# A bank of its own for the gate and up chunks, the last columns in three tiles, and a longer range of shifted ring places

## The chip, the cores and the metric

The kernel runs on one core of a Trainium2 chip. Its time is the device time in microseconds, as the median of the runs. The profile shows one execution, engine by engine: TensorE (PE, its weight loads PEld), VectorE (DVE), ScalarE (ACT), GpSimd (POOL) and the queues that issue transfers (SP, POOL).

## The reference

Two layers work on x, 256 tokens by 1024 columns in float32. Each has a token mixer (a projection to stick-breaking attention, block attention and two gates, a projection of each branch, a merge and an output projection), a residual and a LayerNorm, and then SwiGLU, a residual and a LayerNorm:

```python
def swiglu(x, w_gate, w_up, w_down):
    return (jax.nn.silu(x @ w_gate) * (x @ w_up)) @ w_down

for l in range(DEPTH):
    mix = hybrid_mixer(x, w_in[l], w_branch_sb[l], w_branch_moba[l], w_out[l])
    x = layer_norm(DEEPNORM_ALPHA * x + mix, ln_mix_g[l], ln_mix_b[l])
    ffn = swiglu(x, w_ffn_gate[l], w_ffn_up[l], w_ffn_down[l])
    x = layer_norm(DEEPNORM_ALPHA * x + ffn, ln_ffn_g[l], ln_ffn_b[l])
```

The inner width of SwiGLU is 2816, 22 chunks of 128.

## The kernel before

**Numbers in two parts.** A float32 value is kept as a rounded part (hi) and the remainder (lo), and a product is three matmuls: hi by hi, hi by lo, lo by hi (`mm3`, L493). The weights come in granules of 128 by 1024. For each, a transfer brings it to a buffer called raw, ScalarE's cast writes hi into the ring `whi`, and VectorE's subtraction writes lo into the ring `wlo`. A few granules per layer are loaded into the rings by GpSimd's queue.

**The rings.** Each ring has ten places of 1024 columns (`NSPLIT`); granule g goes to place g mod 10. The table `STATIONARY` (L303) lists ranges of granules whose place begins 16 columns later in `whi` and 48 columns later in `wlo` (`ON`). A granule can only be written when the work that read the last one in its place is done. The granules of layer 1 start at 136: 180 to 183 are its second branch projection (tiles l1pb), where the weights are the stationary operand, and 184 to 191 its output projection (l1pw), where they are the moving one. In layer 0 the same weights are granules 44 to 47 and 48 to 55, and the range (24, 50) holds 44 to 49.

**PSUM.** Eight banks of 512 columns, in three pools with two places each: M and C with one bank a place, B with two. A tile takes a place from its pool once its former tile's readers are done. Waits are kept by tile: a matmul that writes a tile waits for those who read it earlier, in whichever of its halves.

**SwiGLU's main loop.** After eight chunks that are computed ahead, seven rounds follow in each layer. A round computes two more chunks of gate and up (`h_chunk`, 48 matmuls of 256 columns each), and seven products of a 128-by-512 block of the down projection. These are a scheme that replaces eight products by seven; their sums p1, p5, p6 and p7 are combined at the end (`combine_line`), the other three add into `acc[0]` and into the first half of `acc[1]`. The order on TensorE in a round: p1, `acc[0]` twice, the even chunk, p5, p7, `acc[1][:, 0]`, p6, the odd chunk. Both chunks are computed into the same bank, `single`, which is the second half of `acc[1]`. After each chunk ScalarE takes gate and up out of it into a tile called sf (two instructions, in `activated`), and VectorE multiplies them and forms the sums that the products need.

**After the loop** the last chunks of the down projection (eight granules, `TAIL`) are added for tokens 0 to 127 (t = 0) into `acc[0]`, then for t = 1 into `acc[1]`, and a LayerNorm follows for each (`norm_line`, in the last layer `last_norm`). In the last layer, t = 1 goes column piece by column piece: 512 columns in the first half of `acc[1]`, 256 in the second half, 256 in a tile of C. After each piece VectorE adds it to x.

**The order of the work.** A planner in the code (`Weave`) records the instructions of all engines in one run through the program; it sets the place of the side work (weight splits, evacuations) by estimated times. On the chip each engine takes its instructions in that order and waits on semaphores.

Of the kernel before, what the change touches and what calls it, by code (L numbers as in the profile page):

```python
# [14 lines left out]
P = 128  # L15
DEPTH = 2
D = 1024
S = 256
# [8 lines left out]
ALPHA = (2 * DEPTH) ** 0.25  # L27
# [12 lines left out]
class Weave:  # L40
# [12 lines left out]
    def act(self, e, n, f, *args, **kw):  # L53
        f(*args, **kw)  # L54
        self.act_t = max(self.act_t, e) + n / 1200.0 + ACT_FIXED
        return self.act_t + HOP

    def dve(self, e, n, f, *args, **kw):
        f(*args, **kw)  # L59
        self.dve_t = max(self.dve_t, e) + n / 960.0 + DVE_FIXED  # L60
        return self.dve_t + HOP

    def pool(self, e, f, *args, **kw):
        f(*args, **kw)
        self.pool_t = max(self.pool_t, e) + 0.55
        return self.pool_t + HOP
# [38 lines left out]
class WeightStream:  # L105
# [62 lines left out]
    def _place(self, g):  # L168
        if SLOTS[g][0] == B11:
            return "half"  # L170
        if SLOTS[g][0] == B2X:
            return "off"
        return "on" if any(a <= g < b for a, b in STATIONARY) else "off"

# [125 lines left out]
NSPLIT = 10  # L300
ON = (16, 48)
HALF_AT = 256
STATIONARY = ((8, 20), (24, 50), (64, 130), (144, 180), (200, 260))  # L303
TURNED = ("l0sb3", "l1sb3")
N_WARM = 7
LEAD = 4
# [16 lines left out]
def hybrid_trunk_kernel(ctx: ExitStack, tc: tile.TileContext, w, xT_in, x_in, ln_in,  # L323
# [27 lines left out]
    def bankM(name, shape):  # L351
        return psM.tile(shape, F32, tag="M", name=name)

    def bankC(name, shape):
        return psC.tile(shape, F32, tag="C", name=name)

    def bankB(name, shape):
        return psB.tile(shape, F32, tag="B", name=name)

    weave = Weave()  # L360
    taken, left = [0], {}

    def turn(e):

        was = None
        while True:
            k = taken[0] - 2
            if k >= 0 and k not in left:
                yield
            elif (e := max(e, left.get(k, 0.0))) == was:  # L370
                break
            else:
                was = e
                yield e + MARGIN
        taken[0] += 1
        return taken[0] - 1
# [26 lines left out]
    def split_line(hi, lo, src, n, e):  # L403
        e = act(e, n, nc.scalar.copy, hi, src)
        yield e
        return dve(e, n, nc.vector.tensor_sub, lo, src, hi.bitcast(F32))
# [52 lines left out]
    e = dve(3.6, 512, nc.vector.tensor_copy, hi, ws.raw[0][:, first[0]])  # L459
# [39 lines left out]
    def transpose(o, a):  # L499
        nc.tensor.transpose(o, a, ident)  # L500
        weave.t += 0.11

    def pe_after(e):
        weave.t = max(weave.t, e)

    def pe_done():
        return weave.t + HOP
# [53 lines left out]
    def token_out(o, g, t, s_hi, s_lo, first, last):  # L561

        hi, lo = ws.take(g)
        ts = slice(t * P, (t + 1) * P)
        for c0, ps in o:
            cs = slice(c0, c0 + ps.shape[-1])
            mm3(ps, s_hi[:, ts], s_lo[:, ts], hi[:, cs], lo[:, cs], first, last)
# [257 lines left out]
    halves = [slice(h * 512, (h + 1) * 512) for h in range(2)]  # L825

    def residual(e, x, cs, ps, sum_out=None, scale=ALPHA, op=OP.add):
        return dve(e, cs.stop - cs.start, nc.vector.scalar_tensor_tensor, x[:, cs], x[:, cs], scale, ps,
                   op0=OP.mult, op1=op, accum_out=sum_out)

    def scale_shift(e, x, cols, sub, op, scale, g, b, e_scale):

        for c in cols:
            dve(e, c.stop - c.start, nc.vector.scalar_tensor_tensor, x[:, c], x[:, c], sub, g[:, c],
                op0=op, op1=OP.mult)
        for c in cols:
            e = dve(e_scale, c.stop - c.start, nc.vector.scalar_tensor_tensor, x[:, c], x[:, c], scale,
                    b[:, c], op0=OP.mult, op1=OP.add)
            yield c, e

    def norm_line(name, t, junk, gb, scale=ALPHA):

        x = xs[t]
        st = small.tile([P, 2], F32, tag="st", name=f"{name}_st{t}")
        nmu = small.tile([P, 1], F32, tag="nmu", name=f"{name}_nmu{t}")
        ve = small.tile([P, 1], F32, tag="ve", name=f"{name}_ve{t}")
        e = pe_done()
        for h in range(2):
            e = residual(e, x, halves[h], junk[:, h, :], st[:, h:h + 1], scale)
        e = dve(e, 16, nc.vector.tensor_scalar, nmu, st[:, 0:1], st[:, 1:2], -1.0 / D, op0=OP.add, op1=OP.mult)  # L850
        e2 = act(e, D + 100, nc.scalar.activation, junk, x.rearrange("p (h c) -> p h c", h=2), AF.Square,
                 bias=nmu, accum_out=ve)
        e2 = pool(e2, nc.gpsimd.tensor_scalar, ve, ve, 1.0 / D, EPS, op0=OP.mult, op1=OP.add)
        e2 = pool(e2, nc.gpsimd.tensor_tensor, ve, ve, mhalf, op=OP.pow)
        ends = [e for _, e in scale_shift(e, x, halves, nmu, OP.add, ve, *gb, e2)]
        for h in range(2):
            i = yield from turn(ends[h])
            tp = bankC(f"{name}_tp{t}{h}", [P, 4, P])
            pe_after(ends[h])
            for j in range(4):  # L860
                transpose(tp[:, j, :], x[:, (4 * h + j) * P:(4 * h + j + 1) * P])
            ks = slice(h * 4, (h + 1) * 4)
            ts = slice(t * P, (t + 1) * P)
            e = pe_done()
            yield e
            left[i] = xT_ready[t] = yield from split_line(xT_hi[:, ks, ts], xT_lo[:, ks, ts], tp, 512, e)
# [23 lines left out]
    def load_gb(l, i):  # L890
        tiles = []
        for j in range(2):
            a = unit(f"ln{l}{i}{j}", [P, D])
            nc.sync.dma_start(a, ln_in[4 * l + 2 * i + j].partition_broadcast(P))
            tiles.append(a)
        return tiles


    norms = []
    for l in range(DEPTH):  # L900
        G = l * NS_LAYER
        L = f"l{l}"
# [18 lines left out]
        else:  # L921
            for t in range(2):
                weave.finish(norms[:t + 1])
                pe_after(xT_ready[t])
                for j, put in enumerate((put_v, put_q)):
                    ps = bankM(f"{L}pvq{j}{t}", [P, WIDTH])
# [98 lines left out]
        for i in range(4):  # L1025
            ps = bankM(f"{L}pa{i}", [P, 2, S])
# [14 lines left out]
        gb = load_gb(l, 0)  # L1041
# [28 lines left out]
        norms, acc = [], {}  # L1070
        for t, cs in ((0, range(KC)), (1, range(KC))):
            if t not in acc:
                acc[t] = bankB(f"{L}pw{t}", [P, 2, 512])
            for c in cs:
                if t == 0 and c == 4:
                    ws.reach(G + 54)
                    weave.finish(m_sides)
                weave.finish(m_sides[c:c + 1])
                token_out([(512 * h, acc[t][:, h, :]) for h in range(2)], G + 48 + c, t, *m_parts(c),
                          c == 0, c == KC - 1)  # L1080
                if t == 1:
                    ws.allow(G + 48 + NSPLIT + c)
            if c == KC - 1:
                norms.append(weave.start(norm_line(f"{L}a", t, acc[t], gb)))
# [55 lines left out]
        for t in range(2):  # L1140
            weave.finish(norms[:t + 1])
            pe_after(xT_ready[t])
            for j in range(2):
                ps = bankM(f"{L}pft{t}{j}", [P, 512])
# [25 lines left out]
        for c in range(NTOK_FC, LEAD_FC):  # L1170
            h_chunk(c, bankM(f"{L}pf{c}", [P, 2, S]), G + 56 + 2 * c)
        acc = [bankB(f"{L}pd{t}", [P, 2, 512]) for t in range(2)]
        single = acc[1][:, 1, :].rearrange("p (b c) -> p b c", b=2)
        turns = range(taken[0], taken[0] + 2)
        taken[0] += 2
        p1, p6 = (bankC(f"{L}pd{n}", [P, 512]) for n in ("one", "six"))
        p5, p7 = (bankM(f"{L}pd{n}", [P, 512]) for n in ("five", "seven"))

        def combine_line():

# [41 lines left out]


        gb = load_gb(l, 1)
        banks = [[(512 * h, a[:, h, :]) for h in range(2)] for a in acc]
        if l == DEPTH - 1:
            weave.finish(combined)
            banks[1][1:] = [(512, single[:, 0, :]), (768, bankC(f"{L}pe", [P, 512])[:, :256])]

        def h_parts(i):  # L1230
            return [h[:, i % 4, :] for h in (h_tok, h_rest)[i // 4]]

        norms = []
        for t in range(2):
            def down(part, t=t):
                for i in range(len(TAIL)):
                    if i == 6:
                        weave.finish(sides)
                    for c0, ps in part:
                        token_out([(c0, ps)], g + i, t, *h_parts(i), t == 1 and c0 >= 512 and i == 0,  # L1240
                                  i == len(TAIL) - 1)
                    if t == 1:
                        ws.allow(g + i + NSPLIT)
            if l < DEPTH - 1:
                down(banks[t])
                weave.finish(combined)
                norms.append(weave.start(norm_line(f"{L}b", t, acc[t], gb, 1.0)))
            else:
                last_norm(f"{L}b", t, banks[t], gb, down)
        weave.finish(norms[:1])  # L1250
# [85 lines left out]
```

## Time and profile before

| | |
|---|---|
| median of 3 runs | 719.88 us (719.54 to 720.37) |
| profiled execution, its own time | 719.56 us |
| its span | 717.8 us |
| granted TensorE clock, mean | 0.998 |
| busy: PE, PEld | 702.4 us (98%), 641.2 us (89%) |
| busy: DVE, ACT, POOL | 596.6, 424.8, 34.7 us |
| HBM read, written | 148.87 MB, 8.13 MB |

A row of the timeline is: start in us from the span's start, length in us, engine, source line, operation, tile written <- tiles read, shape, and in brackets the engine's idle time just before it with the engine and tile that ended it. Buffer numbers are left out in names, so l0pd is `acc[0]` or `acc[1]` of layer 0 and, in the profile before, also `single`. The tiles of p1, p5, p6 and p7 are l0pdone, l0pdfive, l0pdsix and l0pdseven. A row of the waits is: engine, tile and line that waited, for whom, us in total, times, longest. A row of the chain of waits is: start, length, engine, tile, line. Source line 487 is the helper for all matmuls, 54 and 59 those for ScalarE and VectorE. The length of a matmul includes the pipeline, so the distance between two starts tells TensorE's pace.

### The profile page before, as it was taken

The numbers are of one execution on the slowest core, as the hardware profiler recorded it, in microseconds if no ns is written. First come the engines' busy times: TensorE is split into PE (matmuls) and PEld (weight loads), VectorE is DVE, ScalarE is ACT, GpSimd is POOL, SyncE is SP. The second block draws the span as 40 slices with busy tenths as digits, with TensorE's granted clock in tenths as the row PEclk, the third lists the DMA queues.
The fourth block names the chain that finished last, engine by engine and source line by source line (L and its number), as shares of the span: only waits on it lengthen the run. The fifth ranks groups of instructions, "written<-read, shape, count | busy, mean of one in ns | idle before, by whom it ended". The sixth has DMA issues, their size and how long they took to land.

```text
span 717.8 us, 12728 instructions
## 1 busy us (share of the span) xinstructions
PE 702.4 (98%) x4897; PEld 641.2 (89%) x4897; DVE 596.6 (83%) x887; ACT 424.8 (59%) x651; POOL 34.7 (5%) x48
## 2 busy tenths in 40 slices
PE   9999999999999999999999999999999999999994
PEld 6889999998898888889889889999888999999984
DVE  5999887898888887888588987878879889999855
ACT  5766677755665555565356566677466556666710
POOL 0001110001000000000000111000010000000001
PEclk9999999999999999999999999999999999999999
DMA  8998899876675665657459597995758656656701
GB/s 291 345 332 243 238 243 254 278 275 227 201 244 171 188 199 192 198 194 252 146 177 350 173 255 220 244 277 178 251 196 257 213 168 210 210 176 205 256 9 59
DMA packets 63053, 157.83 MB, mean 220 GB/s; under 512 B 10896, under 2 KB 23184, under 8 KB 62992
## 3 DMA queue, kind: packets, MB, share of 16 engines
q1 hardware_dynamic: 58304, 142.07, 60.0%
q0 software_dynamic: 4544, 14.68, 9.1%
q8 instruction: 38, 0.62, 0.3%
q10 hardware_dynamic: 144, 0.26, 0.1%
q14 instruction: 23, 0.19, 0.1%
HBM read 148.87 MB, written 8.13 MB: 219 GB/s over the span
## 4 chain that ended last, share of the span: by engine, by line
PE 78%; issue 8%; DVE 7%; DMA 3%; ACT 2%; POOL 1%; SPq 1%; POOLq 0%; DVEq 0%; ACTq 0%
PE l1pd L487 15%; PE l0pd L487 10%; PE l1pg L487 6%; PE l0pg L487 6%; DVE wlo L59 3%; PE l0pqk L487 3%; PE l0pw L487 3%; PE l0pft L487 3%; PE l1pw L487 3%; PE l1pft L487 3%; PE l0pf L487 3%; PE l1pf L487 3%; DMA raw<-in_w_dram 3%; PE l1pb L487 2%; PE l0pk L487 2%
## 5 line engine op out<-in xcount | busy, mean ns | idle before, releaser
L59 DVE TENSOR_TENSOR wlo<-raw,whi 128x1024 fp32r<-128x1024 f32 (+1 forms) x262 | 299.0, 1174 | 23.4 <-ACT whi L54 22.3
L54 ACT CAST whi<-raw 128x1024 fp32r<-128x1024 f32 (+1 forms) x261 | 256.7, 1016 | 50.2 <-DVE raw L59 30.3
L487 PE MATMUL l1pd<-xT_hi,whi 128*128 128x256 f32 x224 | 62.1, 277 | 0.0
L487 PE MATMUL l1pd<-xT_hi,wlo 128*128 128x256 f32 x224 | 62.1, 277 | 0.0
L487 PE MATMUL l1pd<-xT_lo,whi 128*128 128x256 f32 x224 | 62.0, 277 | 0.0
L487 PE MATMUL l0pd<-xT_hi,whi 128*128 128x256 f32 x224 | 62.0, 277 | 0.0
L487 PE MATMUL l0pd<-xT_hi,wlo 128*128 128x256 f32 x224 | 62.0, 277 | 0.0
L487 PE MATMUL l0pd<-xT_lo,whi 128*128 128x256 f32 x224 | 62.0, 277 | 0.0
L487 PEld LDWEIGHTS l1pd<-xT_hi,whi 128*128 128x128 f32 x224 | 42.1, 188 | 0.6
L487 PEld LDWEIGHTS l1pd<-xT_lo,whi 128*128 128x128 f32 x224 | 42.1, 188 | 0.6
L487 PEld LDWEIGHTS l0pd<-xT_hi,whi 128*128 128x128 f32 x224 | 42.0, 188 | 0.6
L487 PEld LDWEIGHTS l0pd<-xT_lo,whi 128*128 128x128 f32 x224 | 42.1, 188 | 0.6
L487 PEld LDWEIGHTS l1pd<-xT_hi,wlo 128*128 128x128 f32 x224 | 42.1, 188 | 0.0
L487 PEld LDWEIGHTS l0pd<-xT_hi,wlo 128*128 128x128 f32 x224 | 42.1, 188 | 0.0
L487 PE MATMUL l1pg<-xT_hi,whi 128*128 128x256 f32 x128 | 35.8, 279 | 0.4 <-DVE l1vmb L59 0.4
L487 PE MATMUL l0pg<-xT_hi,whi 128*128 128x256 f32 x128 | 35.7, 279 | 0.0
L487 PE MATMUL l0pg<-xT_hi,wlo 128*128 128x256 f32 x128 | 35.4, 277 | 0.0
L487 PE MATMUL l1pg<-xT_hi,wlo 128*128 128x256 f32 x128 | 35.4, 277 | 0.0
L487 PE MATMUL l0pg<-xT_lo,whi 128*128 128x256 f32 x128 | 35.4, 277 | 0.0
L487 PE MATMUL l1pg<-xT_lo,whi 128*128 128x256 f32 x128 | 35.4, 276 | 0.0
L59 DVE TENSOR_TENSOR l0sf<-l0sf 128x256 f32<-128x256 f32 (+1 forms) x32 | 11.7, 364 | 17.1 <-ACT l0sf L54 16.6
L487 PEld LDWEIGHTS l1pg<-xT_hi,whi 128*128 128x128 f32 x128 | 24.0, 188 | 1.3 <-DVE l1vmb L59 0.9
(487 smaller groups left out, 2028.0 us busy)
## 6 DMA issues: line engine op xcount, KB each, us to landing
raw<-in_w_dram SPq DMA_DIRECT2D x226, 512.0 KB, 4.9
whi<-in_w_dram POOLq DMA_DIRECT2D x14, 512.0 KB, 6.1
wlo<-in_w_dram POOLq DMA_DIRECT2D x14, 512.0 KB, 8.1
ln<-in_ln_dram SPq DMA_DIRECT2D x8, 512.0 KB, 7.3
raw<-in_w_dram SPq DMA_DIRECT2D x7, 256.0 KB, 5.2
l0mb_scr<-l0mb_turn SPq DMA_DIRECT2D x4, 384.0 KB, 6.9
l0mb_turn<-l0mb_scr SPq DMA_DIRECT2D x16, 96.0 KB, 5.2
l1mb_scr<-l1mb_turn SPq DMA_DIRECT2D x4, 384.0 KB, 4.6
```

Of the source, the lines that this page charges most:

```text
L54: f(*args, **kw)
L59: f(*args, **kw)
L487: nc.tensor.matmul(o, a, b, start=start, stop=stop)
```

## The change

`single` becomes an M tile of its own (`bankM`, named pf). p7, which had an M place, goes to the second half of `acc[1]`; p5 stays in M. Before, t = 1 had its second 512 columns in `acc[1]`'s second half; now they are in `single`, in both layers. So `norm_line` is given the two tiles that it reads, and in the last layer the three pieces lie in three tiles. The range (144, 180) becomes (144, 190), so granules 180 to 189 are shifted too.

```diff
-STATIONARY = ((8, 20), (24, 50), (64, 130), (144, 180), (200, 260))
+STATIONARY = ((8, 20), (24, 50), (64, 130), (144, 190), (200, 260))
...
-    def norm_line(name, t, junk, gb, scale=ALPHA):
+    def norm_line(name, t, junk, gb, scale=ALPHA, sums=None):
...
         for h in range(2):
-            e = residual(e, x, halves[h], junk[:, h, :], st[:, h:h + 1], scale)
+            e = residual(e, x, halves[h], sums[h] if sums else junk[:, h, :], st[:, h:h + 1], scale)
...
         acc = [bankB(f"{L}pd{t}", [P, 2, 512]) for t in range(2)]
-        single = acc[1][:, 1, :].rearrange("p (b c) -> p b c", b=2)
+        single = bankM(f"{L}pf", [P, 2, S])
...
-        p5, p7 = (bankM(f"{L}pd{n}", [P, 512]) for n in ("five", "seven"))
+        p5, p7 = bankM(f"{L}pdfive", [P, 512]), acc[1][:, 1, :]
...
-        banks = [[(512 * h, a[:, h, :]) for h in range(2)] for a in acc]
+        flat = single.rearrange("p b c -> p (b c)")
+        banks = [[(0, a), (512, b)] for a, b in ((acc[0][:, 0, :], acc[0][:, 1, :]), (acc[1][:, 0, :], flat))]
         if l == DEPTH - 1:
             weave.finish(combined)
-            banks[1][1:] = [(512, single[:, 0, :]), (768, bankC(f"{L}pe", [P, 512])[:, :256])]
+            banks[1][1:] = [(512, flat[:, :256]), (768, bankC(f"{L}pe", [P, 512])[:, :256])]
...
-                norms.append(weave.start(norm_line(f"{L}b", t, acc[t], gb, 1.0)))
+                norms.append(weave.start(norm_line(f"{L}b", t, acc[t], gb, 1.0, [ps for _, ps in banks[t]])))
```

The order of instructions is the same on every engine. What differs is which tile they name, and which of them wait. Rows of the order name an instruction's line, operation, tile written <- tiles read and shape, and the semaphores of engines that it waits for.

TensorE in the first round of layer 0, from p5's last matmul to the odd chunk's first, before:

```order
L487 MATMUL l0pdfive<-whi,l0hp_lo 128x512
L487 MATMUL l0pdseven<-whi,l0hp_hi 128x512 [waits Activation_49]
L487 MATMUL l0pdseven<-wlo,l0hp_hi 128x512
L487 MATMUL l0pdseven<-whi,l0hp_lo 128x512
L487 MATMUL l0pd_2565<-whi,l0hp_hi 128x512 [waits Activation_49]
L487 MATMUL l0pd_2565<-wlo,l0hp_hi 128x512
L487 MATMUL l0pd_2565<-whi,l0hp_lo 128x512
L487 MATMUL l0pdsix<-whi,l0hp_hi 128x512
L487 MATMUL l0pdsix<-wlo,l0hp_hi 128x512
L487 MATMUL l0pdsix<-whi,l0hp_lo 128x512
L487 MATMUL l0pd_2565<-xT_hi,whi 128x256
```

and with the change:

```order
L487 MATMUL l0pdfive<-whi,l0hp_lo 128x512
L487 MATMUL l0pd_2565<-whi,l0hp_hi 128x512
L487 MATMUL l0pd_2565<-wlo,l0hp_hi 128x512
L487 MATMUL l0pd_2565<-whi,l0hp_lo 128x512
L487 MATMUL l0pd_2565<-whi,l0hp_hi 128x512
L487 MATMUL l0pd_2565<-wlo,l0hp_hi 128x512
L487 MATMUL l0pd_2565<-whi,l0hp_lo 128x512
L487 MATMUL l0pdsix<-whi,l0hp_hi 128x512
L487 MATMUL l0pdsix<-wlo,l0hp_hi 128x512
L487 MATMUL l0pdsix<-whi,l0hp_lo 128x512
L487 MATMUL l0pf<-xT_hi,whi 128x256 [waits Activation_49]
```

The wait on ScalarE has moved from `acc[1][:, 0]`'s product (the fifth row before) to the first matmul of the odd chunk (the last row), six matmuls later. p7 now writes `acc[1]` (2565) too.

TensorE at the boundary of the layers, where t = 1's last sums are followed by layer 1's first two tiles (l1pvq00 and l1pvq10), before:

```order
L487 MATMUL l0pd1_2565<-wlo_99,l0hr_hi_3467 128x512
L487 MATMUL l0pd1_2565<-whi_98,l0hr_lo_3468 128x512
L487 MATMUL l1pvq00_3899<-whi_98,xT_hi_108 128x512 [waits Activation_49]
...
L487 MATMUL l1pvq00_3899<-wlo_99,xT_hi_108 128x512
L487 MATMUL l1pvq00_3899<-whi_98,xT_lo_109 128x512
L487 MATMUL l1pvq10_3929<-whi_98,xT_hi_108 128x512
L487 MATMUL l1pvq10_3929<-wlo_99,xT_hi_108 128x512
```

and with the change (three of l1pvq00's 24 matmuls are shown, the first and the last two):

```order
L487 MATMUL l0pf_2566<-wlo_99,l0hr_hi_3467 128x512
L487 MATMUL l0pf_2566<-whi_98,l0hr_lo_3468 128x512
L487 MATMUL l1pvq00_3899<-whi_98,xT_hi_108 128x512 [waits Activation_49]
...
L487 MATMUL l1pvq00_3899<-wlo_99,xT_hi_108 128x512
L487 MATMUL l1pvq00_3899<-whi_98,xT_lo_109 128x512
L487 MATMUL l1pvq10_3929<-whi_98,xT_hi_108 128x512 [waits DVE_49]
L487 MATMUL l1pvq10_3929<-wlo_99,xT_hi_108 128x512
```

l1pvq00's wait is as before. l1pvq10 now waits for VectorE, whose last read of `single` (l0pf) frees the place in M.

TensorE at the end of layer 1, where the second column piece of t = 1 begins, before:

```order
L487 MATMUL l1pd1_6276<-whi_98,l1hr_hi_7173 128x512
L487 MATMUL l1pd1_6276<-wlo_99,l1hr_hi_7173 128x512
L487 MATMUL l1pd1_6276<-whi_98,l1hr_lo_7174 128x512
L487 MATMUL l1pd1_6276<-whi_98,l1h0_hi_5814 128x256 [waits DVE_49]
L487 MATMUL l1pd1_6276<-wlo_99,l1h0_hi_5814 128x256
L487 MATMUL l1pd1_6276<-whi_98,l1h0_lo_5815 128x256
```

and with the change:

```order
L487 MATMUL l1pd1_6276<-whi_98,l1hr_hi_7173 128x512
L487 MATMUL l1pd1_6276<-wlo_99,l1hr_hi_7173 128x512
L487 MATMUL l1pd1_6276<-whi_98,l1hr_lo_7174 128x512
L487 MATMUL l1pf_6277<-whi_98,l1h0_hi_5814 128x256
L487 MATMUL l1pf_6277<-wlo_99,l1h0_hi_5814 128x256
L487 MATMUL l1pf_6277<-whi_98,l1h0_lo_5815 128x256
```

The piece is written to `single` (l1pf), and the wait on VectorE is gone.

## The prediction

> **What bounds the kernel now.** I read the page's first part, then TensorE's waits, then the chain of waits, and last the timelines where TensorE stops.
>
> ```profile
> PE 702.4 (98%) x4897; PEld 641.2 (89%) x4897; DVE 596.6 (83%) x887; ACT 424.8 (59%) x651; POOL 34.7 (5%) x48
> ...
> PE l0pd L487 <- ACT l0sf L54: 4.8, 6, 1.0
> PE l1pd L487 <- DVE x L59: 1.5, 1, 1.5
> ...
> PE l1pg L487 <- DVE l1vmb L59: 0.4, 1, 0.4
> ```
>
> TensorE is the bound: it is busy for 98% of the span, and apart from the start only two waits are worth money. Six times in layer 0 it waits until ScalarE has evacuated a gate-and-up chunk into l0sf, and once at the very end until VectorE has updated x. Idle time counts from the modelled end of a pipelined matmul, so each wait costs more than that view says; start-to-start times tell the price. First, the layer-0 wait in rounds one and two:
>
> ```profile
> 228.27 0.40 PE L487 MATMUL l0pdseven<-whi,l0hp_lo 128*128 128x512 f32 x1
> 229.69 0.50 PE L487 MATMUL l0pd<-whi,l0hp_hi 128*128 128x512 f32 x1 [1.03 <-ACT l0sf L54]
> 230.03 0.40 PE L487 MATMUL l0pd<-wlo,l0hp_hi 128*128 128x512 f32 x1
> 230.26 0.39 PE L487 MATMUL l0pd<-whi,l0hp_lo 128*128 128x512 f32 x1
> ...
> 245.35 0.40 PE L487 MATMUL l0pdseven<-whi,l0hp_lo 128*128 128x512 f32 x1
> 246.49 0.50 PE L487 MATMUL l0pd<-whi,l0hp_hi 128*128 128x512 f32 x1 [0.75 <-ACT l0sf L54]
> 246.82 0.40 PE L487 MATMUL l0pd<-wlo,l0hp_hi 128*128 128x512 f32 x1
> ```
>
> A 512-column matmul follows the last after 0.23 us (230.03 to 230.26). The waiting one comes after 1.42 us and its successor after 0.34 us, so round one loses 1.76 - 0.46 = 1.30 us; round two loses 1.14 + 0.33 - 0.46 = 1.01 us. What TensorE waits for is seen in the chain of waits:
>
> ```profile
> 224.28 2.35 DVE wlo L59 x2
> 226.63 0.61 DVE raw L59
> 227.26 0.70 DVE raw L59
> ...
> 228.04 1.05 ACT whi L54
> 229.09 0.56 ACT l0sf L54 x2
> ...
> 229.69 0.96 PE l0pd L487 x3
> 230.65 0.69 PE l0pdsix L487 x3
> 231.34 5.51 PE l0pd L487 x48
> 236.88 0.04 issue
> 236.93 0.66 ACT l0sf L54 x2
> 237.61 0.44 DVE l0sf L59
> 238.07 0.43 DVE l0sf L59
> ```
>
> The even chunk's two evacuations stand in ScalarE's queue behind a cast that waits for VectorE's additions. The product acc[1][:, 0] (three matmuls) does not read what they write; it only writes the other half of the tile they read. It has to wait all the same, and p6 and the odd chunk (48 matmuls) stand behind it. Layer 1 does the same work without this wait:
>
> ```profile
> 238.50:322.50 84.00, 80.26 (x586) 74.11 (x585) 71.28 (x94) 49.36 (x73) 0.00 (x0) 1.00 0.58 188
> 591.40:670.40 79.00, 79.00 (x587) 74.55 (x586) 72.01 (x95) 49.38 (x71) 0.00 (x0) 1.00 0.60 200
> ```
>
> Columns: length, then busy time of TensorE, its weight loads, VectorE, ScalarE, GpSimd, granted clock, DMA share, GB/s. Five rounds take 84.0 us in layer 0 and 79.0 us in layer 1: 1.0 us each, as the start-to-start times said. TensorE runs at its full granted clock in both.
>
> **The change part by part.** *The chunk's own bank, in the loop.* The product acc[1][:, 0] loses its wait. The evacuation now holds up only the odd chunk, which really rewrites that bank; its first matmul stands six 512-column matmuls later (two products: 6 x 0.23 = 1.37 us). Is that enough cover? In round one TensorE reaches the odd chunk at 228.27 + 7 x 0.228 = 229.86, and the release that the chain shows is 229.69: 0.17 us to spare. In the others it reaches it at 245.35 + 1.59 = 246.94, against 246.49: 0.45 us. Does the release move when a round gets shorter? The chain runs from the odd chunk's evacuation (236.93) through VectorE's work on it, its splits and additions, and the cast, to the even evacuation, with no step of TensorE in between: from 236.88 to 246.49 it takes 9.6 us, and from there the odd chunk needs 236.88 - 231.18 = 5.7 us (its first matmul is below). A round by this chain is 15.3 us, under the 15.8 us that TensorE needs. So TensorE stays the bound, and the gain is 1.30 + 5 x 1.01 = 6.35 us, taken as 6.3. VectorE's work, 71.3 us in five rounds, fits 79.0 us, as layer 1 shows (72.0). Bounds: 6.4 if no remainder of the wait is left; 2.5 if one more cast of 1.05 us came ahead of each evacuation (0.88 us left in round one, 0.60 in each of the five others).
>
> ```profile
> 230.95 0.39 PE L487 MATMUL l0pdsix<-whi,l0hp_lo 128*128 128x512 f32 x1
> 231.18 0.28 PE L487 MATMUL l0pd<-xT_hi,whi 128*128 128x256 f32 x1
> ```
>
> That the other banks change (p7 into the freed half, p5 into the other M place) costs nothing: p7 is read by VectorE in the combination, and acc[1]'s next write comes after the whole t = 0 pass of 48 matmuls.
>
> *The end.* In the last layer the second third of x's last columns goes into that bank, and no longer waits for VectorE's read of the first:
>
> ```profile
> 702.35 0.39 PE L487 MATMUL l1pd<-whi,l1hr_lo 128*128 128x512 f32 x1
> 704.28 0.39 PE L487 MATMUL l1pd<-whi,l1h_hi 128*128 128x256 f32 x1 [1.55 <-DVE x L59]
> 704.51 0.28 PE L487 MATMUL l1pd<-wlo,l1h_hi 128*128 128x256 f32 x1
> ...
> 703.55 0.68 DVE L59 SCALAR_TENSOR_TENSOR x<-x,l1pd 128x512 f32<-128x512 f32 x1
> 704.26 0.69 DVE L59 BATCH_NORM_STATS2 l1b_bn<-x 128x6 f32<-128x512 f32 x1
> 707.45 0.42 DVE L59 SCALAR_TENSOR_TENSOR x<-x,l1pd 128x256 f32<-128x256 f32 x1 [2.49 <-PE l1pd L487]
> ```
>
> From 702.35 to the second 256-column matmul it takes 2.16 us; without the wait 0.23 + 0.12 = 0.35. VectorE does not take the gain away: it is done with the first piece at 704.95, and the second then comes at about 705.6 instead of 707.45. All that follows moves by 1.8 us.
>
> *The layer boundary.* x's second half of t = 1 is now read from the chunk's bank, an M place, and the next layer's first tiles are M tiles. The order shows that the added wait lies on l1pvq10, 24 matmuls into the layer, not on l1pvq00. VectorE's second read begins at 360.13 and takes 0.69 us; l1pvq10 starts at 364.75.
>
> ```profile
> 359.31 0.39 PE L487 MATMUL l1pvq<-whi,xT_hi 128*128 128x512 f32 x1
> 364.75 0.39 PE L487 MATMUL l1pvq<-whi,xT_hi 128*128 128x512 f32 x1
> ...
> 360.13 0.68 DVE L59 SCALAR_TENSOR_TENSOR x<-x,l0pd 128x512 f32<-128x512 f32 x1
> ```
>
> Cost nothing; the 24 matmuls hide it. Without them it would be 360.82 - 359.31 + 0.11 for the restart = 1.6 us.
>
> *The ring places.* Granules 180 to 189 move by 16 and 48 columns: 180 to 183 are layer 1's l1pb weights (stationary), 184 to 189 the first six of its w_out (moving). Layer 0's l0pb already sits in such places:
>
> ```profile
> 141.50 10.88 PE l0pb L487 x96
> 152.39 17.83 PE l0pw L487 x78
> ...
> 496.91 11.52 PE l1pb L487 x96
> 508.42 18.39 PE l1pw L487 x81
> ```
>
> The same 96 matmuls take 10.88 against 11.52 us: a gain of 0.64. The moving side pays a little. l0pw, with two of its eight granules shifted, runs at 17.83 / 78 = 0.2286 us, l1pw, with none, at 18.39 / 81 = 0.2270; 78 x 0.0016 = 0.12 us for two granules, so about 0.3 for six. Bounds: 0 to 0.4. Net 0.3 gained. The Trainium skill ("SBUF — State Buffer", Specifications) counts operands in lines of 16 bytes; shifts of 64 and 192 bytes keep every start's place in its line, so by that rule nothing moves here and the total is 0.3 us smaller. The rows of l0pb and l1pb differ, and I go by them.
>
> **The sum.** 6.3 + 1.8 + 0.3 = 8.4 us. The profiled execution took 719.56 us (span 717.8), which gives 711.2; the median of the runs is 0.3 above it. I predict 711.3 us.
>
> **The rivals.** *A, the wait only moves.* The chunks of a round still share one bank, so the odd chunk waits for the same evacuation, and only 0.17 to 0.45 us keep them apart. Should the evacuation come a cast later, the loop brings the lower bound of 2.5, the sum is 4.6 and the time 715.3. Against it: the chain of 15.3 us above. The Trainium skill ("Perfetto Trace Analysis", Matmuls) wants independent matmul groups to rotate through banks, so that an evacuation overlaps the next group; by it this rival is what to expect of one bank.
>
> *B, the gain is used up downstream.* TensorE arrives 6.3 us earlier at layer 1, where one wait (0.4 us, l1vmb) shows that VectorE is close behind. If weights bound that stretch, the loop's gain would be spent there and only 1.8 + 0.3 stay: 717.8. Against it: that is the only wait between the two loops, and loads and splits are released by TensorE's progress.
>
> *C, no change.* The waits are for data, not for the tile, and the layout alters nothing but the 0.3 of the ring: 719.6. Against it: the product reads l0hp and the ring, and layer 1, with the same reads, does not wait.
>
> *D, slower.* In layer 0's loop, VectorE and ScalarE become the bound: without TensorE's pause they meet casts that wait for ring places, ahead of the evacuation. The chain must grow from 15.3 us past 16.8 + 2.1 / 6 = 17.2 us before the 2.1 us from elsewhere are eaten; one further whi cast and wlo split in each (1.05 + 1.2 us) make 17.5, so 6 x 0.7 - 2.1 = 2.1 us slower, 722.0. Against it: VectorE is idle for 84.0 - 71.3 = 12.7 us of five rounds, and TensorE frees places earlier, not later.
>
> **How the numbers follow.** Forecast 0.80, A 0.11, B 0.03, C 0.03, D 0.03. The forecast's own range is 710.3 to 712.4 (ring and loop bounds, and 0.4 us between runs). To leave no more than 2 in 10 out I reach into A, as far as an evacuation three quarters of a cast late (0.6 + 5 x 0.34 = 2.3 us left, 713.6): 709.9 to 714.0. A measurement tells about 0.2% (1.4 us) from no change; forecast, A and B lie beyond it: faster 0.94, same 0.03, slower 0.03.
>
> **What would show it.** In the changed profile TensorE's waits hold no wait for l0sf before acc[1]'s product, five layer-0 rounds take 79 us, l1pf follows l1pd in the end without a gap, l1pb takes 10.9 us, and nothing stops before l1pvq. A wait of l0pf's odd chunk on l0sf would show A; a new wait for l1vmb or whi in layer 1, B; rounds over 16.8 us, D. The prediction is wrong if the evacuation falls behind the odd chunk's start.

## The result, and the profile after

The changed kernel takes 711.06 us (median of 4 runs, 710.88 to 711.3), the one before, on the same chip, 719.95 us (4 runs, 719.54 to 720.37). The ratio is 0.9877 with a 95% interval of 0.986 to 0.9894: 8.9 us faster. The prediction was 711.3 us. The profiled execution took 711.3 us, with a span of 709.5 us.

First the page's busy times after, and the first rows of TensorE's waits (engine, tile and line that waited, for whom, us in total, times, longest):

```profile
PE 700.5 (99%) x4897; PEld 642.3 (91%) x4897; DVE 595.9 (84%) x887; ACT 424.2 (60%) x651; POOL 34.7 (5%) x48
```

```profile
PE busy L441 <- DVE mhalf L436: 1.0, 1, 1.0
PE l1pg L487 <- DVE l1vmb L59: 0.3, 1, 0.3
```

Neither the six waits for l0sf nor the wait for x is there, and no row for l0pf or l1pvq has come in their place. What is left is a wait at the start (busy, before the first projection), one of 0.3 us in layer 1, which was 0.4 us before, and one of 0.2 us in the first projection (l0pv, for a cast).

Where did the time go? p1 is the first product of a round, so its first and last starts (two figures after the durations) bound six of the seven rounds. The rows are those of tiles l0pdone, l1pdone and l1pe, before and then after; l1pe is the last column piece.

```profile
L487 PE MATMUL l0pdone<-whi,l0hp_hi x7: 395/395/395, 219.6 to 320.7; 128*128 128x512 f32 x7
...
L487 PE MATMUL l1pdone<-whi,l1hp_hi x7: 395/395/395, 575.5 to 670.2; 128*128 128x512 f32 x7
...
L487 PE MATMUL l1pe<-whi,l1h_hi x4: 283/283/283, 707.2 to 708.3; 128*128 128x256 f32 x4
```

```profile
L487 PE MATMUL l0pdone<-whi,l0hp_hi x7: 395/395/395, 220.1 to 314.9; 128*128 128x512 f32 x7
...
L487 PE MATMUL l1pdone<-whi,l1hp_hi x7: 395/395/395, 569.0 to 663.8; 128*128 128x512 f32 x7
...
L487 PE MATMUL l1pe<-whi,l1h_hi x4: 283/283/283, 699.0 to 700.1; 128*128 128x256 f32 x4
```

| stretch | before, us | after, us | difference |
|---|---|---|---|
| start to the first p1 of layer 0 | 219.6 | 220.1 | +0.5 |
| six rounds of layer 0 | 101.1 | 94.8 | -6.3 |
| from there to the first p1 of layer 1 | 254.8 | 254.1 | -0.7 |
| six rounds of layer 1 | 94.7 | 94.8 | +0.1 |
| from there to l1pe | 37.0 | 35.2 | -1.8 |
| l1pe to the end of the span | 10.6 | 10.5 | -0.1 |

The differences sum to the 8.3 us between the two spans. The 0.5 us at the start is not the change's: it comes before any instruction that the change touches. Other kernels below, with the same instructions there, show 219.7 to 220.6 us for that stretch.

Layer 0's rounds now run as layer 1's do, by the windows view (length, busy time of TensorE, weight loads, VectorE, ScalarE, GpSimd, granted clock, DMA share, GB/s). The first row is five rounds of layer 0, the second five of layer 1:

```profile
238.00:317.00 79.00, 79.00 (x587) 74.56 (x586) 71.22 (x95) 49.11 (x73) 0.00 (x0) 1.00 0.62 203
576.00:655.00 79.00, 79.00 (x588) 74.57 (x587) 71.99 (x96) 49.04 (x70) 0.00 (x0) 1.00 0.61 200
```

The cover in round one, by the timelines of TensorE and ScalarE after:

```profile
230.21 0.39 PE L487 MATMUL l0pdsix<-whi,l0hp_lo 128*128 128x512 f32 x1
230.43 0.28 PE L487 MATMUL l0pf<-xT_hi,whi 128*128 128x256 f32 x1
```

```profile
228.59 1.05 ACT L54 CAST whi<-raw 128x1024 fp32r<-128x1024 f32 x1 [3.23 <-DVE raw L59]
229.55 0.38 ACT L54 ACTIVATE l0sf<-l0pf 128x256 f32<-128x256 f32 x1
229.82 0.36 ACT L54 COPY l0sf<-l0pf 128x256 f32<-128x256 f32 x1
...
245.05 0.38 ACT L54 ACTIVATE l0sf<-l0pf 128x256 f32<-128x256 f32 x1
```

ScalarE has read the bank at 230.18, and the odd chunk's first matmul follows at 230.43, without a gap after p6. ScalarE still waits 3.23 us for VectorE ahead of that cast: it is as late as before, only nobody waits for it. The next even evacuation starts at 245.05, 15.5 us after this one. It ends at 245.68, and the odd chunk of round two starts at 246.21, 0.53 us later; in rounds three to six this distance is the same.

The tail after, on TensorE and on VectorE:

```profile
695.90 0.39 PE L487 MATMUL l1pd<-whi,l1hr_lo 128*128 128x512 f32 x1
696.13 0.28 PE L487 MATMUL l1pf<-whi,l1h_hi 128*128 128x256 f32 x1
```

```profile
697.11 0.68 DVE L59 SCALAR_TENSOR_TENSOR x<-x,l1pd 128x512 f32<-128x512 f32 x1
697.82 0.69 DVE L59 BATCH_NORM_STATS2 l1b_bn<-x 128x6 f32<-128x512 f32 x1
699.20 0.42 DVE L59 SCALAR_TENSOR_TENSOR x<-x,l1pf 128x256 f32<-128x256 f32 x1 [0.69 <-PE l1pf L487]
```

TensorE writes l1pf from 696.13 on, while VectorE reads l1pd only at 697.11. VectorE is through with the first piece at 698.51 and waits 0.69 us for the second.

Last the ring, in the chain of waits (start, length, what):

```profile
490.85 10.88 PE l1pb L487 x96
501.74 18.63 PE l1pw L487 x81
```

96 matmuls of l1pb take 10.88 us instead of 11.52, and 81 of l1pw 18.63 instead of 18.39.

### The profile page after: what moved, and what is told of

It reads as the page before. It is cut to its first block, busy times and chain, and to the rows that moved or that the text cites. A ratio compares the mean times of both kernels' runs of the same rounds, so it can differ in the third digit from the quotient of the medians.

```text
span 709.5 us, 12728 instructions
## 1 busy us (share of the span) xinstructions
PE 700.5 (99%) x4897; PEld 642.3 (91%) x4897; DVE 595.9 (84%) x887; ACT 424.2 (60%) x651; POOL 34.7 (5%) x48
## 4 chain that ended last, share of the span: by engine, by line
PE 96%; DVE 1%; DMA 1%; SPq 1%; issue 0%; POOL 0%; POOLq 0%; ACT 0%; DVEq 0%
PE l0pf L487 15%; PE l1pf L487 14%; PE l1pg L487 6%; PE l0pg L487 6%; PE l0pd L487 5%; PE l1pd L487 5%; PE l1pw L487 3%; PE l0pqk L487 3%; PE l0pw L487 3%; PE l1pqk L487 3%; PE l1pvq L487 3%; PE l0pft L487 3%; PE l1pft L487 3%; PE l1pk L487 2%; PE l0pk L487 2%; PE l0pu L487 2%
## 5 line engine op out<-in xcount | busy, mean ns | idle before, releaser
L487 PE MATMUL l1pf<-xT_hi,whi 128*128 128x256 f32 x288 | 79.8, 277 | 0.0
L487 PE MATMUL l1pf<-xT_hi,wlo 128*128 128x256 f32 x288 | 79.8, 277 | 0.0
L487 PE MATMUL l1pf<-xT_lo,whi 128*128 128x256 f32 x288 | 79.7, 277 | 0.0
L487 PE MATMUL l0pf<-xT_hi,whi 128*128 128x256 f32 x288 | 79.7, 277 | 0.0
L487 PE MATMUL l0pf<-xT_hi,wlo 128*128 128x256 f32 x288 | 79.7, 277 | 0.0
L487 PE MATMUL l0pf<-xT_lo,whi 128*128 128x256 f32 x288 | 79.6, 276 | 0.0
L487 PEld LDWEIGHTS l1pf<-xT_hi,whi 128*128 128x128 f32 x288 | 54.1, 188 | 0.6
L487 PEld LDWEIGHTS l1pf<-xT_lo,whi 128*128 128x128 f32 x288 | 54.2, 188 | 0.6
L487 PEld LDWEIGHTS l0pf<-xT_hi,whi 128*128 128x128 f32 x288 | 54.1, 188 | 0.7
L487 PEld LDWEIGHTS l1pf<-xT_hi,wlo 128*128 128x128 f32 x288 | 54.2, 188 | 0.0
```

Of the source, the lines that this page charges most:

```text
L487: nc.tensor.matmul(o, a, b, start=start, stop=stop)
```

## The experiments

The theory: the waits belong to the tile, not to the half of it that is read; the change moves the wait behind six matmuls of cover, and layer 0's loop, the tail and the ring gain separately. Its rivals are those of the prediction. The two kernels with a late evacuation and the last one below ran beside one set of runs of the kernel before (719.49 us, 7 runs), the others beside another (719.73 us, 13 runs).

**The ring range put back.**

```diff
-STATIONARY = ((8, 20), (24, 50), (64, 130), (144, 190), (200, 260))
+STATIONARY = ((8, 20), (24, 50), (64, 130), (144, 180), (200, 260))
```

> The change with the range of shifted ring places put back to (144, 180); the bank and the tail as in the change. Theory: the range is worth 0.64 us in l1pb (96 matmuls at 0.120 instead of 0.113 us) and costs about 0.24 us in l1pw, as the changed profile shows, so this kernel is 0.4 us slower than the change: 711.5 us, with l1pb back at 11.5 us and l1pw at its pace of before. Rival: the shift does nothing (operands start on the same 16-byte lines either way) and l1pb's pace comes from something else that the change moved: l1pb stays at 10.9 us and the time at 711.1.

Measured: 711.86 us (711.35 to 713.5), ratio 0.9891 [0.9875, 0.9907]. Its chain of waits:

```profile
492.65 11.52 PE l1pb L487 x96
504.16 18.39 PE l1pw L487 x81
```

Both stretches are back at the times of before, so the range is worth 0.64 - 0.24 = 0.40 us. The medians differ by 0.8 us, and the runs lie above those of the changed kernel (711.35 to 713.5 against 710.88 to 711.3), but they scatter over more than the 0.4 us in question: the profiled execution (713.5 us) holds two waits in layer 1, 1.0 us for l1gate and 0.7 us for pp, which the changed profile does not have. The size is taken from the rows.

**The ring range alone**, in the kernel before.

```diff
-STATIONARY = ((8, 20), (24, 50), (64, 130), (144, 180), (200, 260))
+STATIONARY = ((8, 20), (24, 50), (64, 130), (144, 190), (200, 260))
```

> The kernel before with only the range changed to (144, 190). Theory: 0.4 us faster than before, 719.5 us; l1pb 10.9 us, l1pw 0.24 us longer, all seven waits of TensorE as before. Rival (the range has a part in the loop's or the end's gain): more than 1 us faster.

Measured: 719.26 us (10 runs, 719.01 to 720.39), ratio 0.9993 [0.9984, 1.0003]. The interval holds 0.4 us as well as no change, so the times cannot tell; the chain of waits shows the same two steps as with the whole change, and TensorE's waits are those of before (4.8 us for l0sf in six, 1.6 us for x):

```profile
496.93 10.88 PE l1pb L487 x96
507.81 18.63 PE l1pw L487 x81
```

**The tail's second piece back in the shared tile**, the rest of the change kept.

```diff
-            banks[1][1:] = [(512, flat[:, :256]), (768, bankC(f"{L}pe", [P, 512])[:, :256])]
+            banks[1][1:] = [(512, acc[1][:, 1, :256]), (768, bankC(f"{L}pe", [P, 512])[:, :256])]
```

> The change, but in the last layer the second piece of t = 1's columns (512 to 767) goes into the second half of acc[1], which p7 has left, and no longer into the chunk's own bank. Theory (waits go by tile): TensorE again waits for VectorE's read of the first half, 1.8 us, and nothing else changes: 712.9 us. Rival (waits go by bank, or the wait was for VectorE's data): the time stays at 711.1.

Measured: 713.33 us (713.15 to 713.92), ratio 0.9909 [0.9894, 0.9924]. The wait for x is back (1.6 us, idle time), and l1pe starts 700.8 - 663.8 = 37.0 us after the last p1, as before; with the change 35.2:

```profile
L487 PE MATMUL l1pdone<-whi,l1hp_hi x7: 395/395/395, 569.0 to 663.8; 128*128 128x512 f32 x7
...
L487 PE MATMUL l1pe<-whi,l1h_hi x4: 283/283/283, 700.8 to 701.9; 128*128 128x256 f32 x4
```

So the tail is worth 1.8 us by itself; the spans differ by as much (711.3 and 709.5 us), the medians by 2.3. The piece was written to a bank that VectorE did not read at that time; only the tile was the same.

**A late evacuation.** The cover of 0.17 and 0.45 us was the point on which rival A turned. Here ScalarE makes two copies of 128 by 512 ahead of the even chunk's evacuation, in the first five rounds of each layer, into a tile that the evacuation then overwrites.

```diff
-        def activated(name, ps):
+        def activated(name, ps, late=False):
...
+            for _ in range(2 * late):
+                nc.scalar.copy(both.rearrange("p (k c) -> p k c", k=2), xT_hi[:, :2, :].bitcast(F32))
...
-            both, e = activated(name, ps)
+            both, e = activated(name, ps, i >= 4 and i % 2 == 0)
```

> The change, with two extra ScalarE copies of 128x512 (about 0.5 us each, into the tile that the evacuation then writes) ahead of the even chunk's evacuation in the first five rounds of each layer; the order is otherwise the same. It delays the release by about 1.0 us. Theory: in layer 0 the cover of six matmuls leaves 0.17 us in round one and 0.45 in the others, so 0.83 + 4 x 0.55 = 3.0 us are lost, with 0.1 us for each restart 3.5; in layer 1 the odd chunk comes 2 us after the release, so nothing is lost: 714.5 us, and TensorE waits at l0pf's odd chunk for l0sf five times, never at l1pf's. Rival (the evacuation is far from any bound, the cover is larger than worked out): 711.1 us. Rival (no cover at all): 5.0 us in layer 0 alone, 716 us or more.

Measured: 716.26 us (715.94 to 716.53), ratio 0.9949 [0.9932, 0.9965]. Six rounds of layer 0, then round one on ScalarE and TensorE, and the wait:

```profile
L487 PE MATMUL l0pdone<-whi,l0hp_hi x7: 395/395/395, 220.6 to 320.0; 128*128 128x512 f32 x7
```

```profile
229.07 1.05 ACT L54 CAST whi<-raw 128x1024 fp32r<-128x1024 f32 x1 [3.23 <-DVE raw L59]
230.03 1.27 ACT L1104 COPY l0sf<-xT_hi 128x512 f32<-128x512 f32 x2
231.33 0.38 ACT L54 ACTIVATE l0sf<-l0pf 128x256 f32<-128x256 f32 x1
...
230.69 0.39 PE L487 MATMUL l0pdsix<-whi,l0hp_lo 128*128 128x512 f32 x1
232.03 0.38 PE L487 MATMUL l0pf<-xT_hi,whi 128*128 128x256 f32 x1 [0.95 <-ACT l0sf L54]
```

```profile
PE l0pf L487 <- ACT l0sf L54: 3.4, 5, 1.0
```

The wait stands at the odd chunk, as rival A has it. The evacuation starts 2.26 us after the cast's start, against 0.96 us in the changed kernel: 1.30 us later, not the 1.0 us that was expected. In the four other rounds it is 1.25 us, counted from p1 to the evacuation's end. Less the cover, and with 0.11 us for each restart, this makes (1.30 - 0.17 + 0.11) + 4 x (1.25 - 0.45 + 0.11) = 4.9 us; the six rounds take 99.4 us instead of 94.8, 4.6 more. With no cover the same sum would be 6.9 us. The time alone would mislead: 716.26 us is 1.8 us more than expected and lies where the rival without cover was put (716 us or more), because the delay was larger than expected and, in the profiled execution, the loop began 0.5 us later (a wait of 1.1 us for a cast in the first projection). The rows decide: the cover is about as large as the prediction had it, and rival A is a real limit that this kernel does not reach. Layer 1's rounds do not change: there ScalarE is idle for about 1.5 us ahead of that evacuation, and the copies fit in.

**The same late evacuation in the kernel before.**

> The kernel before with the same extra copies ahead of the even chunk's evacuation in the first five rounds of each layer. Theory: the wait at acc[1]'s product has no cover left, so layer 0 loses the whole 1.0 us in five rounds, 5.0 us, and in layer 1, where the product comes 0.6 us after the release, 0.4 us and a restart of 0.1 in each of five, 2.5 us: 727.4 us. Rival (the product waits for something else than the evacuation): 720.0 us.

Measured: 730.2 us (728.62 to 731.01), ratio 1.0141 [1.0124, 1.0158], 2.8 us more than expected. The six rounds of layer 0 take 112.0 us instead of 101.1:

```profile
L487 PE MATMUL l0pdone<-whi,l0hp_hi x7: 395/395/395, 219.9 to 331.9; 128*128 128x512 f32 x7
```

Five delays of 1.30 us explain 6.5 of these 10.9 us. Rounds four to six tell the rest, on TensorE's timeline (p7's last matmul, then the one that waits) and by three windows of 3.40 us, behind the waits of rounds one, four and five (granted clock third from the right). The first two rows are p6's in round one:

```profile
232.31 0.63 PE L487 MATMUL l0pdsix<-whi,l0hp_hi 128*128 128x512 f32 x1
232.74 0.63 PE L487 MATMUL l0pdsix<-wlo,l0hp_hi 128*128 128x512 f32 x1
...
286.20 0.40 PE L487 MATMUL l0pdseven<-whi,l0hp_lo 128*128 128x512 f32 x1
288.59 0.51 PE L487 MATMUL l0pd<-whi,l0hp_hi 128*128 128x512 f32 x1 [1.99 <-ACT l0sf L54]
...
305.84 0.40 PE L487 MATMUL l0pdseven<-whi,l0hp_lo 128*128 128x512 f32 x1
308.23 0.50 PE L487 MATMUL l0pd<-whi,l0hp_hi 128*128 128x512 f32 x1 [1.99 <-ACT l0sf L54]
...
323.88 0.40 PE L487 MATMUL l0pdseven<-whi,l0hp_lo 128*128 128x512 f32 x1
```

```profile
231.93:235.33 3.40, 3.40 (x14) 3.01 (x13) 2.93 (x4) 2.31 (x3) 0.00 (x0) 0.50 0.69 205
289.96:293.36 3.40, 3.40 (x17) 3.30 (x16) 3.05 (x3) 1.51 (x2) 0.00 (x0) 0.50 0.65 245
308.24:311.64 3.40, 3.40 (x23) 3.15 (x24) 3.17 (x5) 2.78 (x3) 0.00 (x0) 1.00 0.58 171
```

From p7 to p7 round four takes 19.64 us and round five 18.04 us, after the same pause of 2.39 us. Behind the one pause TensorE was granted half the clock for 3.4 us, behind the other the full clock. So the further 1.6 us of round four are a slower clock. Rounds one and two lost it as well (p6's matmuls follow each other by 0.43 us in round one, not 0.23), round three did not. Without it a round is 18.04 - 16.8 = 1.24 us longer than before: 5 x 1.24 + 3 x 1.6 = 11.0 us, against 10.9. The expectation's loss in layer 1 did not come either, for the idle time of ScalarE named above.

**The wait put at p7.** Here the chunks share a tile with p7: they use `acc[1]`'s second half, p7 its first half, and the product that was in `acc[1]` goes to M.

```diff
-        single = bankM(f"{L}pf", [P, 2, S])
+        single = acc[1][:, 1, :].rearrange("p (b c) -> p b c", b=2)
...
-        p5, p7 = bankM(f"{L}pdfive", [P, 512]), acc[1][:, 1, :]
+        p5, third = (bankM(f"{L}pd{n}", [P, 512]) for n in ("five", "seven"))
+        p7 = acc[1][:, 0, :]
...
-            product(acc[1][:, 0, :], j, 5, w, 0)
+            product(third, j, 5, w, 0)
```

> The chunk's bank is again the second half of acc[1], as before, but the tile's first half holds p7, and the third accumulating product has the tile in M that p7 had before (in the last layer its first piece too). The only difference to the kernel before in the loop is which product shares the tile with the chunk: p7 stands three matmuls nearer to the chunk than the accumulating product. Theory (waits go by tile): p7's product waits for the evacuation, and each of six rounds in layer 0 loses 3 x 0.23 = 0.68 us more than before, 4.1 us in all; in layer 1 the release (about 0.7 us after the chunk's end) just meets p7, so 0 to 0.1 us in each of seven rounds; the end does not wait, 1.8 us gained. The range is the changed one, 0.4 us gained. 721.9 us, and 722.5 at most. Rival (the product waited for data, or the loss lay in two engines working in neighbouring banks): as before in the loop, 717.8 us.

Measured: 726.19 us (725.75 to 726.97), ratio 1.0087 [1.0072, 1.0102]. TensorE's waits, and the six rounds of each layer:

```profile
PE l0pd L487 <- ACT l0sf L54: 8.9, 6, 1.7
...
PE l1pd L487 <- DVE l1comb L59: 0.8, 1, 0.8
PE l0pd L487 <- DVE l0comb L59: 0.8, 1, 0.8
```

```profile
L487 PE MATMUL l0pdone<-whi,l0hp_hi x7: 395/395/395, 219.7 to 324.8; 128*128 128x512 f32 x7
...
L487 PE MATMUL l1pdone<-whi,l1hp_hi x7: 395/395/395, 580.4 to 677.1; 128*128 128x512 f32 x7
```

In layer 0 six rounds take 105.1 us, 4.0 more than before: 0.67 us a round, the three matmuls (3 x 0.23) by which the wait moved forward. That is the theory's figure, and it shows that the wait goes where the tile's next writer stands. Two sizes were missed, and they are most of the 4.3 us by which the time exceeds the expected 721.9. Layer 1's rounds are 0.33 us longer each (96.7 against 94.7 us): with only p5 as cover the evacuation is a little too late even where nothing delays it.

```profile
588.42 0.39 PE L487 MATMUL l1pdfive<-whi,l1hp_lo 128*128 128x512 f32 x1
588.86 0.51 PE L487 MATMUL l1pd<-whi,l1hp_hi 128*128 128x512 f32 x1
589.20 0.39 PE L487 MATMUL l1pd<-wlo,l1hp_hi 128*128 128x512 f32 x1
```

The two steps are 0.44 and 0.34 us instead of 0.23 each: 0.32 us, of which the waits view shows no row, since the pause lies within the modelled end of the matmul ahead. And once in each layer the last odd chunk waits for the combination, which reads p7 in the other half: a further wait by tile, which nobody had counted.

**Only the stationary granules shifted.**

```diff
-STATIONARY = ((8, 20), (24, 50), (64, 130), (144, 190), (200, 260))
+STATIONARY = ((8, 20), (24, 50), (64, 130), (144, 184), (200, 260))
```

> The change with the range ending at 184, where layer 1's l1pb weights end, so that l1pw's granules stay unshifted. Theory: l1pw is back at its pace of before (0.24 us gained), but granule 183's shifted place runs 16 and 48 columns into the place of 184, which can then only be written after l1pb's last matmul: a cast (1.05 us), a split (1.2 us) and two releases, about 2.4 us of wait before l1pw: 713.2 us. Rival (the planner's order has enough other work there, or the write is late anyway): 710.8 us, the best of the ranges.

Measured: 710.97 us (710.59 to 711.4), ratio 0.9877 [0.9862, 0.9892]. The theory's wait did not come, and the time is the rival's (710.8); chain of waits, and ScalarE's casts at the start of l1pb:

```profile
490.73 10.88 PE l1pb L487 x96
501.61 18.39 PE l1pw L487 x81
```

```profile
490.79 2.00 ACT L54 CAST whi<-raw 128x1024 fp32r<-128x1024 f32 x2
```

The first of these two casts is granule 184, by the order of ScalarE's instructions. It writes from column 4 x 1024 = 4096 on; granule 183 sits in 3 x 1024 + 16 = 3088 to 4112, and its last columns are read only by the last matmuls of l1pb, shortly before 501.6 us. The kernel's limit on splits (`allow`) knows the case of a shifted granule that reaches into the next place, not that of an unshifted one written over its predecessor's end. So by these places and times 16 columns of granule 183's hi part (and 48 of its lo part) are written over before they are read, where the theory had expected a wait. This is worked out from the code and the order; the trace shows no columns. As a kernel it is no candidate, but its time can be read: with the six moving granules unshifted l1pw is back at 18.39 us. The 0.24 us are theirs.

## Why the prediction was right

**Loop, 6.3 us predicted, 6.3 measured.** The rounds went to layer 1's length, and the cover held: the odd chunk followed 0.25 us after the end of the evacuation in round one and 0.53 us in rounds two to six. Less the 0.04 us that the release took in the kernel before, this is 0.2 and 0.5 us of cover, where 0.17 and 0.45 had been worked out, and the late evacuation paid about what these leave over. The step that the chain of ScalarE and VectorE is shorter than TensorE's round, so that the release keeps up when the rounds shrink, is borne out too: the first two even evacuations are 15.5 us apart, of which 0.2 us is the time that the odd chunk came later than its release, so the chain itself takes the 15.3 us of the prediction.

**Tail, 1.8 us predicted, 1.8 measured,** in the changed kernel and by its undoing.

**Boundary, 0 predicted, 0 seen.** VectorE's second read ends at 354.95 us, l1pvq's 24 first matmuls run on until about 358.9, and no wait of l1pvq is in the list. The timeline of VectorE after:

```profile
354.27 0.68 DVE L59 SCALAR_TENSOR_TENSOR x<-x,l0pf 128x512 f32<-128x512 f32 x1
```

**Ring, 0.3 us predicted, 0.40 measured.** The gain of 0.64 was exact. The cost was taken as 0.3 and is 0.24 us: six granules at 0.04 us, where l0pw's two had suggested 0.06. The Trainium skill ("SBUF — State Buffer", Specifications) has operands read in lines of 16 bytes; by the lines alone shifts of 64 and 192 bytes would change nothing. With the range alone l1pb went from 11.52 to 10.88 us and l1pw from 18.39 to 18.63, so the lines are not all that counts, in either direction.

**The sum.** The terms give 8.4 us and the spans 8.3, but that these meet is in part luck: 0.5 us of scatter at the start stood against the change, while the stretch between the loops took 0.7 us less, of which the ring explains 0.4. The medians differ by 8.9. The prediction's last step does not follow from its own numbers: the profiled execution less 8.4 is 711.2 us, and with the 0.3 us by which the median lies above it 711.5, not 711.3. The changed kernel's median lies 0.2 us below its profiled execution, and that 711.3 came so near to 711.06 is luck by these amounts.

**The rivals.** A's mechanism is real, and the experiment with the late evacuation prices it, but the evacuation is not that late here. The Trainium skill ("Perfetto Trace Analysis", Matmuls) asks for independent groups to rotate through banks; six matmuls of other work between two uses of one bank served here as well. B: from the last p1 of layer 0 to the first of layer 1 nothing was given back (254.1 against 254.8 us). C: the same data are read, and the wait is gone. D: the rounds are 15.8 us, and VectorE is busy 71.22 of 79.00 us.

## What to carry to other kernels

Where waits are kept by tile, two banks in one tile are one lock: whoever writes the one half waits for the reader of the other, so things that are written and read at different times should be tiles of their own. Price a wait that moves by the work that stands between the reader and the next writer, less how late the reader is, and measure both start to start, since pauses shorter than a matmul's modelled end are in no row of the waits. A shift of operands in memory can be worth a small sum, but look at every reader: the one that gained 0.64 us for stationary operands cost 0.24 us for moving ones.

## What the runs showed of the hardware that was not expected

- **The clock after a pause.** In the kernel before with the late evacuation, TensorE paused five times for 2.0 to 2.3 us (idle time). Three of these pauses were followed by 3.41 us at a granted clock of 0.50, in which the matmuls ran at about half pace (0.43 us instead of 0.23), 1.6 us lost each. The half clock began at 231.92, 252.40 and 289.95 us, that is 6 and 11 steps of 3.41 us apart, and the step of 3.41 us ahead of each of these times holds its whole pause, to within 0.04 us. Carried on, the same steps have a boundary at 269.47 and one at 307.01 us. These cut the other two pauses (268.56 to 270.55 and 306.24 to 308.23 us), which left the clock at 1.00. In these five cases the place of the pause among the steps tells the two kinds apart; the length does not, since two pauses of 1.99 us had it and two did not. Shorter pauses, up to 1.7 us with the wait at p7 and 1.0 us in the loop of the kernel before, left the clock at 1.00. The Trainium skill ("TensorE: Matmul & The Clock Gate", What's actually happening) puts the half clock after an idle window of about 3.4 us that runs freely; the window and its free running agree with the steps here, but the window need not be idle from end to end: 2.0 us in one of them were enough.
- **Where the ring begins matters.** 256-column matmuls with stationary operands at the place's start follow each other by 11.52 / 96 = 0.120 us, shifted by 16 and 48 columns by 10.88 / 96 = 0.113 us. For 512-column matmuls with moving operands it is 18.39 / 81 = 0.227 us unshifted and 18.63 / 81 = 0.230 us with six of eight granules shifted. Why is open; no run here tells whether it is the weight loads and the matmuls meeting at the memory.
- **A restart costs about 0.11 us.** In the waits of the kernel before and in the one shown with the wait at p7, the second matmul comes after 0.33 to 0.34 us, not 0.23; the prediction had it in its terms. With the wait at p7, pauses of 0.21 us and such restarts made each round of layer 1 0.32 us longer, where the waits view showed nothing.
